# First pass over the weights of k and q: four token tiles of values taken along, weights loaded in pieces, zeros multiplied at the start, first sums copied before the values

## Chip, core and metric

The kernel runs on one core of a Trainium2 chip. A core has five engines that run side by side and wait for each other through semaphores: TensorE (PE, matrix products into PSUM), VectorE (DVE), ScalarE (ACT), GpSimd (POOL) and SyncE (SP, which here only issues transfers). Each engine works through its own queue strictly in order. The metric is the device time of one execution in microseconds (us), lower is better; the figure used is the median of several runs.

## What is computed

One transformer block on 1024 tokens of width 1024, in float32. Only its beginning matters here: a norm, a wide projection, and what the projection's columns are for.

```python
h = rmsnorm(x, g_mix_pre[l])
proj = h @ w_in[l]
qa, ka, va, gate_a, beta_a, alpha_a, qb, kb, vb = jnp.split(proj, split_at, axis=-1)
out_a = gated_deltanet(qa, ka, va, gate_a, beta_a, alpha_a, ...)
out_b = dilated_attention(qb, kb, vb, rel_bias)
mix = jnp.concatenate([out_a, out_b], axis=-1) @ w_out[l]
x = x + rmsnorm(mix, g_mix_post[l])
```

After it comes a gated feed-forward part, which isn't touched.

## The kernel before

**How a product is made.** TensorE gets float32 accuracy from rounded operands: each operand is split into a high part and a low part, and `mm3` adds three products, high by high, high by low and low by high. So each block of weights and of activations is first cast (ACT, the high part) and then subtracted (DVE, the low part). In the names of the profile `wr` is a raw weight block, `w` its parts, `xT` a raw block of the transposed input, `hTh` and `hTl` its parts after multiplication with the norm's gain `gT`. The factor of each token's norm, `rtok`, is put on after the product.

**The first stage.** The depth of 1024 has eight blocks (`KT` = 8, index k). The tokens have two halves of 512 (`hf`), or eight tiles of 128 (t). `proj_first(hf)` runs over k and multiplies block k of the tokens of one half with two chunks of weights, those of head 0 of k and of q (`order[0]` and `order[1]`); their sums stand in the two banks of the pool `pj`. `proj_v(0, tiles)` then makes the values (`bv0`, 256 columns plus 8 columns `wba` for beta and alpha) of four token tiles, each summed over all k in a bank of the pool `pt`, which has four banks and is called `tp` in the profile. The order on TensorE is: half 0 of k and q, value tiles 0 to 3, half 1 of k and q, value tiles 4 to 7, and after that the other chunks.

**What leaves the banks.** `raw_sink(raw, True)` copies a sum of k or q from `pj` to `raw` on ACT, gives the bank back, and later multiplies with `rb` (the norm's factors as a row). A value tile's sink multiplies with `rtok` on ACT (`vs`, `bp`), gives the bank back and stores. `norm_in(t)` makes `rtok`: it squares a tile of x (`xn`, three buffers) on ACT with the sum as a by-product, takes the power on POOL, and after four tiles transposes the four columns on TensorE into a bank of `pt`.

**Loads.** `load_w` is one strand, and all of its transfers are issued by SP in the order in which it yields them: the weights of k and q and the eight `xT` of half 0, `wba`, four blocks of weights for the values, `ident`, four `xn`, the eight `xT` of half 1, and the rest. Raw weights stand in four buffers (`rawS`), `xT` in six. A transfer that needs a buffer waits on SP until that buffer has been used up, and all later transfers wait behind it.

**What sets the order.** A planner (`Weaver`) takes all open strands and always issues the instruction that can start first by its own table of costs; ties go to the strand's priority. `After` holds back a strand until the planner expects its data. `Either` lets the planner choose between two engines. A strand's `slack` tells how long before TensorE would run dry an instruction must be ready by the planner's reckoning to be put into TensorE's queue ahead of others. So the order in each queue is fixed when the kernel is built, and a change at one place can move instructions elsewhere.

Of the kernel before, what the change touches and what calls it, by code (L numbers as in the profile page):

```python
# [48 lines left out]
LATE = 2000.0  # L49
PB = 2  # L50
SW = 832

FAR = {2: 256, 3: 576, 4: 448, 5: 416, 6: 256, 7: 576}
PWO = (2, 3, 2)
# [158 lines left out]
class After:  # L213


    def __init__(self, *aps, late=0.0):
        self.aps, self.late = aps, late


class Strand:  # L220
# [16 lines left out]
class Weaver:  # L237
# [125 lines left out]
    def run(self, *until):  # L363
        while not all(e.set for e in until):
# [15 lines left out]
            for s in live:  # L380
                if s.alts is not None:
                    s.req = s.alts[0]
                    if s.ver >= 0:
                        s.req = min(s.alts, key=lambda r: self.finish(s, r, live))
                names = [x.tensor.name for x in s.req.aps] if isinstance(s.req, After) else \
                    [x[0] for op in s.req for x in op.ins + op.outs]
                v = sum(self.ver.get(n, 0) for n in names)
                if v != s.ver:
                    s.ver = v
                    if isinstance(s.req, After):  # L390
                        s.data = max([t for x in s.req.aps for t, _ in self.wr.get(x.tensor.name, {}).values()] + [0.0])
                    else:
                        s.data = max(self.when(op) for op in s.req)
                if isinstance(s.req, After):
                    s.start, s.safe = s.data + s.req.late, True
                else:
                    free = self.clock[s.req[0].eng]
                    s.start = max(free, s.data, self.port if s.req[0].port else 0.0)
                    if s.req[0].eng == "PE":
                        s.start = max(s.start, self.rest.get(s.gen.__name__, 0.0) if s.pace else 0.0)  # L400
                    if s.req[0].table not in (None, self.table) and not s.eager:
                        s.start += TABLE
                    s.safe = s.req[0].eng != "PE" or s.data + s.slack <= free
                first = min(first, s.start)
# [137 lines left out]
def block_kernel(ctx: ExitStack, tc: tile.TileContext, a, out):  # L542
# [107 lines left out]

    def load_w():

        first = chunks(order[0]) + chunks(order[1])
        got = {c: [] for c in first}
        evs = {c: [Event() for _ in range(2)] for c in first}
        for i in range(2):
            for n, c in enumerate(first):
                wr = yield rawS.get([P, 4, P], F32, name="wr")
                yield SY.dma_start(wr[:], a["w_in"][c][:, 4 * i:4 * i + 4, :])
                got[c].append(wr)  # L660
                evs[c][i].fire()
                if not i:
                    w.spawn(prep_w(c, got[c], evs[c]), 1)
                yield from load_xt(4 * i + n, 0)
                if not i and not n:
                    yield SY.dma_start(gT[:], a["g_mix_pre_t"])
            for k in (2, 3):
                yield from load_xt(4 * i + k, 0)
        yield SY.dma_start(wba[:], a["w_ba"])
        yield from load_item(order[2])  # L670
        yield SY.dma_start(ident[:], a["c_ident"])
        for t in range(4):
            yield from load_x(t)
        for k in range(KT):
            yield from load_xt(k, 1)
        for t in range(4, NT):
            yield from load_x(t)
        ev_x.fire()
        for item in order[3:]:
            yield from load_item(item)  # L680

    def load_item(item):
        for c in chunks(item):
            z, evs = [], [Event() for _ in range(2)]
            for i in range(2):
                wr = yield rawS.get([P, 4, P], F32, name="wr")
                yield SY.dma_start(wr[:], a["w_in"][c][:, 4 * i:4 * i + 4, :])
                z.append(wr)
                evs[i].fire()
            w.spawn(prep_w(c, z, evs), 1)  # L690

    ev_x = Event()
    ev_wh = {(c, i): Event() for c in loaded for i in range(2)}

    def prep_w(c, raw, got):
        hi, lo = [], []
        for i in range(4):
            if c in (24, 25):
                z = yield wS.get([P, 2, WB], F32R, name="w")
            else:  # L700
                z = yield wS.get([P, 4, P], F32R, name="w")
            (lo if i % 2 else hi).append(z)
        wts[c] = hi, lo
        for i, (wh, wl) in enumerate(zip(hi, lo)):
            yield got[i]
            wr = raw[i]
            if c in (24, 25):

                k = 4 * (c - 24) + 2 * i
                yield After(wba[:])  # L710
                yield from split_sb(wh[:, :, 256:], wl[:, :, 256:], wba[:, k:k + 2, :])
                wh, wl, wx = wh[:, :, 0:256], wl[:, :, 0:256], wr[:].rearrange("p (k x) c -> p k (x c)", x=2)
            else:
                wh, wl, wx = wh[:], wl[:], wr[:]
            yield After(wr[:])
            yield from split_sb(wh, wl, wx)
            rawS.put(wr)
            ev_wh[c, i].fire()
        loaded[c].fire()

    def proj_first(hf, sinks):
# [3 lines left out]
        for _ in cs:  # L725
            z = yield pj.get([P, 512], F32, name="pj")
            ps.append(z)
        for k in range(KT):
            for c, z in zip(cs, ps):
                yield ev_wh[c, k // 4]  # L730
                yield ev_xt[k, hf]
                wh, wl = wts[c]
                yield mm3(z[:], wh[k // 4][:, k % 4, :], wl[k // 4][:, k % 4, :], *h_of(k, hf * 512, 512),
                          k == 0, k == KT - 1)
        if hf:
            wS.slots = wS.slots[:8]
            for c in cs:
                wS.put(*wts[c][0], *wts[c][1])
        return [w.spawn(sink(hf, z), 1) for sink, z in zip(sinks, ps)]

    def proj_half(c, hf, sink):
        yield loaded[c]
# [9 lines left out]
    def proj_qk(c0, m, ev):  # L752
# [12 lines left out]
        for hf in range(2):  # L765
            yield from proj_half(c0 + m, hf, sink)

    def proj_v(m, tiles=range(NT)):
        c0 = 24 + 2 * m
        yield loaded[c0]  # L770
        yield loaded[c0 + 1]
        wc = [wts[c0], wts[c0 + 1]]
        n = 256 if m else WB

        def sink(t, ps, bank):
            vs = yield outS.get([P, 4, 64], F32, name="vs")
            yield ev_r[t]
            r = rtok[:, t:t + 1]
            yield A.activation(vs[:], ps[:, 0:256].rearrange("p (h d) -> p h d", h=4), AF.Copy, scale=r)
            if not m:  # L780
                yield A.activation(bp[:, :, t], ps[:, 256:WB], AF.Copy, scale=r)
            (pj if m else pt).put(bank)
            yield SY.dma_start(d_v[t, :, 4 * m:4 * m + 4, :], vs[:])
            outS.put(vs)
            ev_v[m][t].fire()
        for t in tiles:
            if m:
                bank = ps = yield pj.get([P, n], F32, name="pj")
            else:
                bank = yield pt.get([P, 4, P], F32, name="tp")  # L790
                ps = bank[:].rearrange("p k j -> p (k j)")[:, 0:n]
            for k0 in range(0, KT, 2):
                ops = []
                wh, wl = (z[k0 % 4 // 2] for z in wc[k0 // 4])
                for k in (k0, k0 + 1):
                    h, l = (z[:, k % 2, :] if not m else z[:].rearrange("p (k x) c -> p k (x c)", x=2)[:, k % 2, :]
                            for z in (wh, wl))
                    ops += mm3(ps[:], *h_of(k, t * P, P), h, l, k == 0, k == KT - 1)
                yield ops
                if t == NT - 1:  # L800
                    wS.put(wh, wl)
            w.spawn(sink(t, ps, bank), 1)
        if not m and tiles[-1] == NT - 1:
            w.spawn(beta_alpha(ev_v[0]), 2)

# [415 lines left out]
    def raw_sink(raw, early=False):  # L1221
        def sink(hf, ps):
            z, f = raw[0][:, 3 + hf * 512:3 + hf * 512 + 512], rb[:, hf * 512:hf * 512 + 512]
            if early:
                yield A.copy(z, ps[:])
                pj.put(ps)
                yield ev_rb[hf]
                yield Either(*[e.tensor_tensor(z, z, f, ALU.mult) for e in (V, G)])
# [21 lines left out]
    def main():  # L1250
# [5 lines left out]
        for hf in range(2):  # L1256
            evs = yield from proj_first(hf, [raw_sink(raw, True) for raw, _ in pair])
            for (_, ev), e in zip(pair, evs):
                ev.append(e)
            yield from proj_v(0, range(4 * hf, 4 * hf + 4))  # L1260
        ev_v0.fire()
        for n, (kind, i) in enumerate(order):
            if kind in ("k", "q", "v"):
# [30 lines left out]
    with ExitStack() as s0:  # L1294
# [10 lines left out]
        def prep_xt(k, hf, x):  # L1305
# [5 lines left out]
            px.put(x)  # L1311
            ev_xt[k, hf].fire()

        def load_x(t):
            x = yield px.get([P, D], F32, name="xn", bufs=3)
            yield SY.dma_start(x[:], a["x"][t * P:(t + 1) * P, :])
            done_in.append(w.spawn(norm_in(t, x), 1))

        def norm_in(t, x):
            ss = px.tile([P, 1], F32, name="ss%d" % t)  # L1320
# [16 lines left out]
        w.spawn(issue(V.memset(mhalf[:], -0.5)), 0)  # L1337
        wS.more(px, "pw", 8)
        w.spawn(load_w(), 2)
        w.spawn(load_consts(), 3)  # L1340
        ev_main = w.spawn(main(), 9)
        w.run(ev_x)
# [1090 lines left out]
```

## Time and profile before

| what | value |
|---|---|
| median of 3 runs | 1210.13 us (1209.64 to 1210.61) |
| time of the profiled execution | 1212.98 us |
| its span, first to last instruction | 1211.2 us, 19599 instructions |
| TensorE busy | 1194.7 us, 99% of the span |
| VectorE busy | 901.5 us, 74% |
| ScalarE busy | 545.9 us, 45% |
| GpSimd busy | 161.2 us, 13% |
| TensorE's share of the chain that ended last | 85% |

The chain that ended last is found by going back from the last instruction, each time to what released it. TensorE carries most of it. The instructions of a group that sit on it back to back are merged to one row with a count.

### The profile page before, as it was taken

How to read it: one execution, taken by the hardware profiler on the slowest of the kernel's cores; microseconds unless marked ns; L12 is line 12 of the kernel's file. 1: busy time of each engine (PE TensorE's matmuls, PEld its weight loads, DVE VectorE, ACT ScalarE, POOL GpSimd, SP SyncE). 2: the span in 40 equal slices, each digit the busy share in tenths (PEclk: the TensorE clock that was granted, in tenths of full speed). 3: DMA queues.
4: the chain of work that ended last, by engine and by line, in shares of the span. 5: the costliest groups of instructions: out<-in, count | busy, mean ns of one | idle time of the engine just before them, and what ended most of it. 6: DMA issues, size and time to landing. Idle time of an engine off the chain costs nothing.

```text
span 1211.2 us, 19599 instructions
## 1 busy us (share of the span) xinstructions
PE 1194.7 (99%) x7101; PEld 992.5 (82%) x7101; DVE 901.5 (74%) x1729; ACT 545.9 (45%) x1065; POOL 161.2 (13%) x140
## 2 busy tenths in 40 slices
PE   7999999999999999999999999999999999999997
PEld 6978898888888878888788888888888888888886
DVE  4689969636786866676998786787667867876886
ACT  6654531235775764454643333333333344544541
POOL 0143410001111200010101110011100100001111
PEclk9999999999999999999999999999999999999999
DMA  7645363667455344784444433332233239644335
GB/s 257 220 138 181 105 166 109 137 212 272 145 202 187 121 157 161 251 263 164 137 151 139 131 122 122 131 109 69 93 122 122 79 120 338 212 146 140 101 118 208
DMA packets 152216, 192.51 MB, mean 159 GB/s; under 512 B 29960, under 2 KB 77832, under 8 KB 152120
## 3 DMA queue, kind: packets, MB, share of 16 engines
q1 hardware_dynamic: 147896, 189.17, 48.5%
q10 hardware_dynamic: 4224, 2.10, 0.6%
q8 instruction: 56, 0.92, 0.3%
q14 instruction: 40, 0.33, 0.1%
HBM read 135.36 MB, written 59.66 MB: 161 GB/s over the span
## 4 chain that ended last, share of the span: by engine, by line
PE 85%; DVE 7%; DMA 4%; issue 2%; ACT 1%; POOL 1%; SPq 0%; DVEq 0%; POOLq 0%; ACTq 0%
PE bank L286 48%; PE pj L286 21%; PE tp L286 4%; PE p L286 3%; PE pw L286 3%; PE pm L286 2%; PE pS L286 2%; PE pV L286 2%; DVE yc L286 1%; DVE x L286 1%; DMA d_x<-x 1%; DVE wbl L286 1%; DMA ks<-d_k 0%; DMA mx<-d_mix 0%; DMA wraw<-in_w_up 0%
## 5 line engine op out<-in xcount | busy, mean ns | idle before, releaser
L286 PE MATMUL pj<-hTh,w 128*128 128x512 f32 x768 | 263.4, 404 | 6.3 <-ACT hTh L286 6.3
L286 PEld LDWEIGHTS pj<-hTh,w 128*128 128x128 f32 x768 | 145.7, 190 | 40.6 <-ACT hTh L286 6.3
L286 ACT CAST wbh<-wraw 128x512 fp32r<-128x512 f32 x129 | 79.7, 621 | 197.2 <-PE bank L286 116.0
L286 PE MATMUL pj<-hTl,w 128*128 128x512 f32 x384 | 151.5, 395 | 0.0
L286 DVE TENSOR_TENSOR wbl<-wraw,wbh 128x512 fp32r<-128x512 f32 x131 | 92.5, 709 | 29.3 <-ACT wbh L286 29.3
L286 PE MATMUL bank<-views 128*128 128x512 f32 (+1 forms) x307 | 84.8, 384 | 0.0
L286 PEld LDWEIGHTS pj<-hTl,w 128*128 128x128 f32 x384 | 73.1, 190 | 12.7 <-DVE hTl L286 0.5
L286 PE MATMUL bank<-views,dah 128*128 128x512 f32 (+1 forms) x214 | 73.5, 379 | 0.0
L286 PE MATMUL bank<-dbh,views 128*128 128x512 f32 (+1 forms) x201 | 70.3, 380 | 0.0
L286 PEld LDWEIGHTS bank<-views 128*128 128x128 f32 x307 | 57.5, 188 | 11.5
L286 POOL TENSOR_TENSOR m<-m,m 128x512 f32<-128x512 f32 x18 | 28.3, 1572 | 256.3 <-DVE r L286 152.4
L286 ACT CAST w<-wr 128x512 fp32r<-128x512 f32 x55 | 33.8, 620 | 47.8 <-PE pj L286 38.8
L286 PE MATMUL bank<-dbh,dah 128*128 128x512 f32 (+1 forms) x129 | 49.1, 381 | 0.0
L286 DVE SCALAR_TENSOR_TENSOR yc<-raw,convw,yc 128x1024 f32<-128x1024 f32 x36 | 46.5, 1292 | 0.5
L286 PEld LDWEIGHTS bank<-views,dah 128*128 128x128 f32 x214 | 40.0, 188 | 7.7
L286 DVE TENSOR_TENSOR w<-wr,w 128x512 fp32r<-128x512 f32 x42 | 29.1, 700 | 21.9 <-ACT w L286 20.7
L286 PE MATMUL pw<-woh,mh 128*128 128x512 f32 x112 | 44.9, 401 | 0.0
L286 PE MATMUL pw<-woh,ml 128*128 128x512 f32 x112 | 43.8, 391 | 0.0
L286 PE MATMUL pw<-wol,mh 128*128 128x512 f32 x112 | 43.7, 390 | 0.0
L286 PEld LDWEIGHTS bank<-dbh,views 128*128 128x128 f32 x201 | 37.7, 188 | 7.1
L286 DVE TENSOR_TENSOR m<-bank,m 128x512 f32<-128x512 f32 x44 | 30.1, 685 | 17.8 <-PE bank L286 17.6
L286 ACT ACTIVATE Sr<-Sr,mx 128x384 f32<-128x384 f32 (+3 forms) x64 | 38.1, 597 | 9.1 <-DVE mx L286 8.7
(379 smaller groups left out, 3085.6 us busy)
## 6 DMA issues: line engine op xcount, KB each, us to landing
wr<-in_w_in SPq DMA_DIRECT2D x56, 256.0 KB
wraw<-in_w_gate SPq DMA_DIRECT2D x52, 256.0 KB
wraw<-in_w_up SPq DMA_DIRECT2D x52, 256.0 KB
views<-d_hid SPq DMA_DIRECT2D x47, 256.0 KB
db<-in_w_down SPq DMA_DIRECT2D x40, 256.0 KB
da<-d_hid SPq DMA_DIRECT2D x30, 256.0 KB
d_hid<-x SPq DMA_DIRECT2D x22, 256.0 KB
d_hid<-r SPq DMA_DIRECT2D x22, 256.0 KB
```

The costliest lines, as they stand in the source:

```text
L286: op.fn(*op.args, **op.kw)
```

## The change

It has four parts, all in the first 60 us of the program.

1. `proj_first(0)` takes four banks of `pt` at its beginning, and after every second k it also adds that pair's products for value tiles 0 to 3. The value tiles are so summed along with k and q, and the four banks are held all the while. Value tiles 4 to 7 follow after `proj_first(1)`. The strand of the value sinks becomes a function of its own (`v_sink`), spawned after the sinks of k and q.
2. `load_w` loads the weights of k and q in pieces of two k (128x256 instead of 128x512, each with its own event, cast and subtraction), in the order in which the pass needs them, with a block of the values' weights after every second k, and `gT` and `wba` early. `After(..., part=True)` lets a strand wait for one piece of a buffer only.
3. `warm` writes zeros into part of `junk` and multiplies them ten times, 512 columns each, into a bank of `pt` that it takes and gives back.
4. The first sums may be copied by DVE as well as by ACT (`Either`). The strands of `norm_in` get a slack of 5000, which keeps their transposes back on TensorE until they are surely ready.

```diff
+SPREAD = 5000.0
...
-    def __init__(self, *aps, late=0.0):
+    def __init__(self, *aps, late=0.0, part=False):
...
+        yield SY.dma_start(gT[:], a["g_mix_pre_t"])
         first = chunks(order[0]) + chunks(order[1])
...
+        for k in range(0, KT, 2):
+            i, j = k // 4, k % 4
             for n, c in enumerate(first):
+                if not j:
+                    wr = yield rawS.get([P, 4, P], F32, name="wr")
+                    got[c].append(wr)
+                yield SY.dma_start(got[c][i][:, j:j + 2, :], a["w_in"][c][:, k:k + 2, :])
+                evs[c][i][j // 2].fire()
...
+                yield from load_xt(k + n, 0)
+            if not k:
+                yield SY.dma_start(wba[:], a["w_ba"])
+            c = vs[i]
+            wr = yield rawS.get([P, 4, P], F32, name="wr")
+            got[c].append(wr)
+            yield SY.dma_start(wr[:], a["w_in"][c][:, 2 * j:2 * j + 4, :])
...
     def proj_first(hf, sinks):
...
+        vs = []
+        if not hf:
+            for t in range(4):
+                z = yield pt.get([P, 4, P], F32, name="tp")
+                vs.append(z)
         for k in range(KT):
             for c, z in zip(cs, ps):
-                yield ev_wh[c, k // 4]
+                yield ev_wh[c, k // 2]
...
+            if vs and k % 2:
+                yield ev_wh[24 + k // 4, k % 4 - 1]
+                for t, z in enumerate(vs):
+                    yield v_ops(0, t, v_rows(0, z), k - 1)
...
-        return [w.spawn(sink(hf, z), 1) for sink, z in zip(sinks, ps)]
+        evs = [w.spawn(sink(hf, z), 1) for sink, z in zip(sinks, ps)]
+        for t, z in enumerate(vs):
+            w.spawn(v_sink(0, t, v_rows(0, z), z), 1)
+        return evs
...
-                yield A.copy(z, ps[:])
+                yield Either(A.copy(z, ps[:]), V.tensor_copy(z, ps[:]))
                 pj.put(ps)
...
-            yield from proj_v(0, range(4 * hf, 4 * hf + 4))
+        yield from proj_v(0, range(4, NT))
...
+        def warm():
+            tp = yield pt.get([P, 4, P], F32, name="tp")
+            yield V.memset(junk[:, 0:512], 0.0)
+            yield [mm(tp[:].rearrange("p k j -> p (k j)"), junk[:, 0:P], junk[:, 0:512]) for _ in range(10)]
+            pt.put(tp)
...
-            done_in.append(w.spawn(norm_in(t, x), 1))
+            done_in.append(w.spawn(norm_in(t, x), 1, SPREAD))
...
+        w.spawn(warm(), 0)
```

From about the end of value tile 7 on, the five engines' queues hold the same instructions in the same order in both kernels. What moves stands ahead of that.

The first place is ACT's queue where the pass over half 0 ends. Before, the copies of the first sums (`raw<-pj`) stand ahead of the first squares of x (`junk<-xn`) and of all products `hTh` of half 1:

```order
L286 CAST w<-wba 128x2x8
L286 COPY raw<-pj 128x512
L286 CAST w<-wr 128x2x256
L286 COPY raw<-pj 128x512
L286 ACTIVATE junk,ss_267<-xn 128x1024
L286 ACTIVATE junk,ss_273<-xn 128x1024
L286 ACTIVATE vs<-tp,rtok 128x256
```

In the changed kernel the one copy that is left on ACT stands behind four squares and behind all eight `hTh` of half 1:

```order
L287 CAST w<-wr 128x2x256
L287 ACTIVATE junk,ss_300<-xn 128x1024
L287 ACTIVATE junk,ss_311<-xn 128x1024
L287 ACTIVATE junk,ss_319<-xn 128x1024
L287 ACTIVATE junk,ss_365<-xn 128x1024
L287 ACTIVATE hTh<-xT,gT 128x512 x8
L287 COPY raw<-pj 128x512
L287 ACTIVATE vs<-tp,rtok 128x256
L287 ACTIVATE bp<-tp,rtok 128x8
```

The copy moved behind the loads of half 1, and the squares moved ahead of the copy. The other copy stands on DVE behind its eight `hTl`.

The second place is SP's queue between the first weights and the second half. In the changed kernel, at the fourth pair of k (`wr` here is in turn a piece for k, a piece for q and a block for the values):

```order
L287 DMA wr<-in_w_in 128x512
L287 DMA wr<-in_w_in 128x256
L287 DMA xT<-in_x_t 128x512
L287 DMA wr<-in_w_in 128x256
L287 DMA xT<-in_x_t 128x512
L287 DMA wr<-in_w_in 128x512
L287 DMA ident<-in_c_ident 128x128
L287 DMA xn<-in_x 128x1024 x4
L287 DMA xT<-in_x_t 128x512 x8
L287 DMA xn<-in_x 128x1024 x3
```

Before, the values' four blocks stood together behind all `xT` of half 0, and stores of values stood between the `xT` of half 1:

```order
L286 DMA xT<-in_x_t 128x512 x3
L286 DMA wba<-in_w_ba 128x64
L286 DMA wr<-in_w_in 128x512 x4
L286 DMA ident<-in_c_ident 128x128
L286 DMA xn<-in_x 128x1024 x4
L286 DMA xT<-in_x_t 128x512 x2
L286 DMA d_v<-vs 128x256
L286 DMA xT<-in_x_t 128x512 x4
```

The stores left the gaps between the `xT` of half 1, and the weights of the values moved ahead, between those of k and q; four transfers more are issued in all, the eight pieces that stand for four blocks.

The third place is TensorE's queue where half 1 begins, in the changed kernel (the last products of value tile 3, then the first three of k, the transposes of the norms' factors, then q):

```order
L287 MATMUL tp<-w,hTl 128x264
L287 MATMUL pj<-hTh,w 128x512
L287 MATMUL pj<-hTl,w 128x512
L287 MATMUL pj<-hTh,w 128x512
L287 MATMUL tp<-ident,rtok 128x128 x4
L287 MATMUL pj<-hTh,w 128x512
L287 MATMUL pj<-hTl,w 128x512
```

Before, the transposes stood among the products of value tile 3, and the whole of four value tiles stood between the two passes over k and q; now the second pass follows the first with only the last pair's value products between them.

More of the change, by code (lines that the diff above doesn't have):

```diff
@@ L213 @@
 class After:
-    def __init__(self, *aps, late=0.0):
-        self.aps, self.late = aps, late
+    def __init__(self, *aps, late=0.0, part=False):
+        self.aps, self.late, self.part = aps, late, part
 class Strand:
@@ L390, in run @@
                     if isinstance(s.req, After):
-                        s.data = max([t for x in s.req.aps for t, _ in self.wr.get(x.tensor.name, {}).values()] + [0.0])
+                        own = [self.region(x) if s.req.part else (x.tensor.name, -1, -1) for x in s.req.aps]
+                        s.data = max([t for n, q, f in own for (p, g), (t, _) in self.wr.get(n, {}).items() if p & q and f & g] + [0.0])
                     else:
@@ L651, in load_w @@
     def load_w():
+        yield SY.dma_start(gT[:], a["g_mix_pre_t"])
         first = chunks(order[0]) + chunks(order[1])
-        got = {c: [] for c in first}
-        evs = {c: [Event() for _ in range(2)] for c in first}
-        for i in range(2):
-            for n, c in enumerate(first):
[L658 to L662, printed above, removed]
-                    w.spawn(prep_w(c, got[c], evs[c]), 1)
[L664 to L670, printed above, removed]
+        vs = chunks(order[2])
+        got = {c: [] for c in first + vs}
+        evs = {c: [[Event() for _ in range(2)] for _ in range(2)] for c in first}
+        for c in vs:
+            evs[c] = [[Event()] for _ in range(2)]
+        for k in range(0, KT, 2):
+            i, j = k // 4, k % 4
+            for n, c in enumerate(first):
+                if not j:
[4 more added lines that the diff above has]
+                if not k:
+                    w.spawn(prep_w(c, got[c], evs[c]), 1)
+                yield from load_xt(k + n, 0)
+            if not k:
+                yield SY.dma_start(wba[:], a["w_ba"])
[3 more added lines that the diff above has]
+            yield SY.dma_start(wr[:], a["w_in"][c][:, 2 * j:2 * j + 4, :])
+            evs[c][j // 2][0].fire()
+            if not j:
+                w.spawn(prep_w(c, got[c], evs[c]), 1)
         yield SY.dma_start(ident[:], a["c_ident"])
@@ L683, in load_item @@
         for c in chunks(item):
-            z, evs = [], [Event() for _ in range(2)]
+            z, evs = [], [[Event()] for _ in range(2)]
             for i in range(2):
@@ L688, in load_item @@
                 z.append(wr)
-                evs[i].fire()
+                evs[i][0].fire()
             w.spawn(prep_w(c, z, evs), 1)
     ev_x = Event()
-    ev_wh = {(c, i): Event() for c in loaded for i in range(2)}
+    ev_wh = {(c, i): Event() for c in loaded for i in range(4)}
     def prep_w(c, raw, got):
@@ L704, in prep_w @@
         for i, (wh, wl) in enumerate(zip(hi, lo)):
-            yield got[i]
+            yield got[i][0]
             wr = raw[i]
@@ L714, in prep_w @@
                 wh, wl, wx = wh[:], wl[:], wr[:]
-            yield After(wr[:])
-            yield from split_sb(wh, wl, wx)
+            for j, ev in enumerate(got[i]):
+                yield ev
+                x = (slice(None), slice(2 * j, 2 * j + 2) if len(got[i]) > 1 else slice(None))
+                yield After(wx[x], part=len(got[i]) > 1)
+                yield from split_sb(wh[x], wl[x], wx[x])
+                ev_wh[c, 2 * i + j].fire()
             rawS.put(wr)
-            ev_wh[c, i].fire()
         loaded[c].fire()
@@ L766, in proj_qk, with v_rows, v_ops, v_sink @@
             yield from proj_half(c0 + m, hf, sink)
+    def v_rows(m, bank):
+        return bank if m else bank[:].rearrange("p k j -> p (k j)")[:, 0:WB]
+    def v_ops(m, t, ps, k0):
+        c0 = 24 + 2 * m
+        ops = []
+        wh, wl = (z[k0 % 4 // 2] for z in wts[c0 + k0 // 4])
+        for k in (k0, k0 + 1):
+            h, l = (z[:, k % 2, :] if not m else z[:].rearrange("p (k x) c -> p k (x c)", x=2)[:, k % 2, :]
+                    for z in (wh, wl))
+            ops += mm3(ps[:], *h_of(k, t * P, P), h, l, k == 0, k == KT - 1)
+        return ops
+    def v_sink(m, t, ps, bank):
+        vs = yield outS.get([P, 4, 64], F32, name="vs")
+        yield ev_r[t]
+        r = rtok[:, t:t + 1]
+        yield A.activation(vs[:], ps[:, 0:256].rearrange("p (h d) -> p h d", h=4), AF.Copy, scale=r)
+        if not m:
+            yield A.activation(bp[:, :, t], ps[:, 256:WB], AF.Copy, scale=r)
+        (pj if m else pt).put(bank)
+        yield SY.dma_start(d_v[t, :, 4 * m:4 * m + 4, :], vs[:])
+        outS.put(vs)
+        ev_v[m][t].fire()
     def proj_v(m, tiles=range(NT)):
@@ L771, in proj_v @@
         yield loaded[c0 + 1]
[L772 to L785, printed above, removed]
         for t in tiles:
             if m:
-                bank = ps = yield pj.get([P, n], F32, name="pj")
+                bank = yield pj.get([P, 256], F32, name="pj")
             else:
                 bank = yield pt.get([P, 4, P], F32, name="tp")
-                ps = bank[:].rearrange("p k j -> p (k j)")[:, 0:n]
+            ps = v_rows(m, bank)
             for k0 in range(0, KT, 2):
[L793 to L799, printed above, removed]
+                yield v_ops(m, t, ps, k0)
                 if t == NT - 1:
-                    wS.put(wh, wl)
-            w.spawn(sink(t, ps, bank), 1)
+                    wS.put(*(z[k0 % 4 // 2] for z in wts[c0 + k0 // 4]))
+            w.spawn(v_sink(m, t, ps, bank), 1)
         if not m and tiles[-1] == NT - 1:
```

## Prediction

> **What bounds the kernel now.** I read the page first, then the chain that ended last, cut to its first 60 us, then the time lines of TensorE and ACT there, and the table by windows.
>
> ```profile
> span 1211.2 us, 19599 instructions
> PE 1194.7 (99%) x7101; PEld 992.5 (82%) x7101; DVE 901.5 (74%) x1729; ACT 545.9 (45%) x1065; POOL 161.2 (13%) x140
> ...
> 1.64 3.84 DMA gT<-in_g_mix_pre_t
> ...
> 5.57 0.73 ACT hTh L286
> 6.30 0.04 issue
> 6.34 14.44 PE pj L286 x48
> 20.78 12.09 PE tp L286 x100
> 32.87 10.89 PE pj L286 x48
> 43.76 12.08 PE tp L286 x100
> 55.84 5.45 PE pj L286 x24
> ```
>
> TensorE is busy for 99% of the span, so an edit pays only by starting TensorE earlier, by making it faster, or by not stopping it. The chain shows where it loses at the head: nothing runs before 6.34, because the transfer of `gT`, issued third, lands at 5.48 and the first `hTh` follows. From 6.34 on TensorE never stops: 48 products of half 0, four value tiles, 48 of half 1, four value tiles, and at 55.84 the next chunk. But 48 equal products take 14.44 the first time and 10.89 the second. The time line of TensorE shows why (start, duration, instruction):
>
> ```profile
> 7.72 1.05 PE L286 MATMUL pj<-hTh,w 128*128 128x512 f32 x2
> ...
> 9.00 1.05 PE L286 MATMUL pj<-hTh,w 128*128 128x512 f32 x2
> ...
> 12.84 0.66 PE L286 MATMUL pj<-hTh,w 128*128 128x512 f32 x2
> ...
> 19.03 0.61 PE L286 MATMUL pj<-hTh,w 128*128 128x512 f32 x2
> 19.48 0.39 PE L286 MATMUL pj<-hTl,w 128*128 128x512 f32 x1
> 19.71 0.61 PE L286 MATMUL pj<-hTh,w 128*128 128x512 f32 x2
> ```
>
> Three products take 1.28 us (7.72 to 9.00) until 12.84, and 0.68 (19.03 to 19.71) after it. So TensorE ran at about half rate for its first 6.5 us, some 15 products at 0.43 instead of 0.23, which cost 3.1 us. The granted clock of the page shows full speed there; the durations tell it.
>
> **The change, part by part.** The products stay the same; only their order and their start differ. So I ask when half 1 of k and q may begin: that is 32.87 before, and everything behind it follows back to back. Before, the four transposes of the norms' factors stood ahead of that point; now they stand behind the first three products of half 1:
>
> ```profile
> 30.08 0.60 PE L286 MATMUL tp<-ident,rtok 128*128 128x128 f32 x4
> 30.44 0.49 PE L286 MATMUL tp<-w,hTh 128*128 128x264 f32 x2
> ```
>
> They take 0.36 (30.08 to 30.44), so the figure to beat is 32.87 - 0.36 = **32.5 us**.
>
> *Earlier start and zeros.* `gT` goes to the front, and half a block of weights comes with it. Memsets and the first issues stand at 0.7 to 0.9 us, so the zeros can begin at about 1.4; ten of them at the 0.43 of the slow rows take 4.3 us, until 5.7. The first data should be ready near that: `gT` issued first is bounded by the first block's 3.33 below (issue 0.73, 2.6 us for 64 times the bytes) and, above, by its own 5.48 now. I take 5.7 for the first real product, at the price of nothing if the data comes later than that, and of up to 1 us if it is ready at 4.7.
>
> *The pass itself.* At full rate it needs 48 x 0.227 = 10.9 us, and the four value tiles 12.09 - 0.36 = 11.7 (their row of the chain has the transposes in it): 22.6 in all, so 28.3 if nothing waits. I add 0.5 for the first pair of k, where the values' first block must be landed, cast and subtracted behind those of k and q: **28.8 us**. Should the slow rate last as long as before (6.5 us from 1.4, so until 7.9), half of 7.9 - 5.7 is lost, 1.1 us: 29.9.
>
> [...]
>
> *The new wait.* The two banks of `pj` hold the sums of half 0, and half 1 writes the same banks. Before, four value tiles (12 us) lay between, and the copies, the first at 20.14, were hidden under them. Now only the last pair's values lie between, a quarter of 11.7, 2.9 us. And the copies no longer come at once: ACT's stands in its queue behind four squares and all eight `hTh` of half 1, DVE's behind the eight `hTl`. So half 1 can't start before **the last `xT` of half 1 has landed and been worked on**. What that means in time, from ACT, DVE and SP:
>
> ```profile
> 3.33 0.62 ACT L286 CAST w<-wr 128x512 fp32r<-128x512 f32 x1 [1.32 <-DMA wr<-in_w_in]
> ...
> 20.14 0.59 ACT L286 COPY raw<-pj 128x512 f32<-128x512 f32 x1 [3.48 <-PE pj L286]
> ...
> 21.62 1.07 ACT L286 ACTIVATE junk<-xn 128x1024 bf16<-128x1024 f32 x1
> ...
> 34.42 1.34 ACT L286 ACTIVATE hTh<-xT,gT 128x512 fp32r<-128x512 f32 x2
> ```
> ```profile
> 34.38 2.73 DVE L286 SCALAR_TENSOR_TENSOR hTl<-xT,gT,hTh 128x512 fp32r<-128x512 f32 x4
> ...
> 61.57 0.63 DVE L286 TENSOR_TENSOR raw<-pj,rb 128x512 f32<-128x512 f32 x1
> ```
> ```profile
> 13.78 9.36 SPq L286 DMA_DIRECT2D xn<-in_x  x4
> 23.18 0.92 SPq L286 DMA_DIRECT2D xT<-in_x_t  x2
> ```
> ```profile
> 1.00:9.00 8.00, 2.66 (x5) 1.78 (x6) 2.80 (x4) 3.76 (x6) 0.00 (x0) 1.00 0.80 236
> 9.00:14.00 5.00, 5.00 (x15) 3.96 (x14) 4.43 (x7) 4.90 (x8) 0.00 (x0) 1.00 1.04 395
> 14.00:20.00 6.00, 6.00 (x28) 4.94 (x27) 3.17 (x9) 2.22 (x8) 0.00 (x0) 1.00 0.94 325
> 20.00:24.50 4.50, 4.50 (x36) 4.38 (x35) 1.00 (x3) 4.33 (x10) 0.83 (x2) 1.00 0.23 44
> 24.50:33.00 8.50, 8.50 (x72) 8.46 (x71) 3.19 (x7) 6.65 (x13) 1.68 (x4) 1.00 0.93 308
> ```
>
> (The windows' last column is GB/s, the one before it the share of the DMA engines.) There are two ways to work it out.
>
> By bytes: until the last `xT` of half 1 the queue moves 16 blocks of 256 KB, four `xn` of 512 KB, eight `xT` and 0.1 MB of small things, 8.5 MB. At the measured rates 1.9 MB are in by 9 us, 3.9 by 14, and the other 4.6 MB take 14.2 us at 325 GB/s or 14.9 at 308: 28.2 to 28.9. Behind it come one `hTh` (0.73) and one copy (0.59): 29.5 to 30.2, if SP never stops.
>
> By shifting the trace: the last `hTh` of half 1 ends at 35.76 now. In its way was a hole: ACT waited 3.48 us for TensorE with the copy at its head, so the squares began at 21.62 and the fourth `xn`, which needs the first one's buffer, and all `xT` behind it were issued late (SP's row of 9.36 us). From 20 to 24.5 only 44 GB/s moved; at 308 that stretch is worth 3.9 us. In the changed kernel the squares stand ahead of the copy, so this hole closes: 35.76 - 3.9 = 31.9, and with the copy 32.5.
>
> SP adds stops of its own, which the first way leaves out: raw weights have four buffers, now filled in turn for k, q and the values, and from the thirteenth transfer on four of them wait for a subtraction on DVE, with every `xT` behind them on the one queue. One such wait costs at least nothing (others are still in flight) and at most a whole trip, 2.6 us from issue (0.73) to use (3.33). I add 1 us for all four, nearer to nothing, because the transfers issued before a stop go on moving through it. That is 30.5 to 31.2 by bytes and 32.5 by shifting; I take **31.3 us** for the first product of half 1. DVE's copy (nearest row 0.63) comes later than ACT's by one subtraction, 2.73 / 4 = 0.7 us; the three products of k and the transposes ahead of q (0.68 + 0.36) cover that.
>
> So the gain is 32.5 - 31.3 = **1.2 us**, where the earlier start alone would give 3.7.
>
> *The rest.* Smaller pieces cost ACT and DVE four more casts and subtractions each, between 0.3 and 0.7 us apiece; the 3.48 us in which ACT waited hide them, and without that cover they stand in the wait above. Value tiles 4 to 7 need banks that are free long before. Behind 55.84 the queues are the same, TensorE waits next to nothing:
>
> ```profile
> PE pm L286 <- DVE rhd L286: 1.0, 1, 1.0
> PE tp L286 <- ACT ys L286: 0.2, 1, 0.2
> ```
>
> These are all its waits from 56 to 300 us. DVE, which is late there, starts its convolutions no later than TensorE's shift, so I carry the gain through unchanged.
>
> **The rivals.** *No new wait (TensorE's work decides).* If the transfers ran at the 395 GB/s of 9 to 14 us to the end, the other 4.6 MB would take 11.6 us, and the copies would be done at 27; then 28.8 or 29.9 holds, a gain of 3.7 to 2.6 us, 1206.4 to 1207.5. Against it: the trace shows that rate only for 5 us.
>
> *Slower.* SP's stops at the four weight buffers decide. Half 1 starts later than before if the last `xT` lands after 31.2 (32.5 less 0.73 and 0.59), so two full trips of 2.6 on the 28.2 to 28.9 are enough: copies done at 34.7 to 35.4, 2.2 to 2.9 us later than now, about 1212.7. For it: each wait is on an engine that itself waits for a transfer. Against it: transfers in flight cover much of a trip.
>
> *The zeros don't do it.* If zeros do not count as work, or TensorE's waits in the first pair keep its clock down, the slow stretch runs on for 6.5 us from 5.7 and costs 3.1 again: 28.8 + 3.1 = 31.9, a gain of 0.6, 1209.5. It shows little, since the copies come at the same time.
>
> **How the numbers follow.** The profiled execution took 1212.98 us around its span of 1211.2, 2.85 more than the median of 1210.13; the gain of 1.2 goes on either: 1211.8 of a profiled execution, **1208.9** as the median. Chances: the new wait with part of the gain 0.62, no new wait 0.24, slower 0.10, zeros without effect 0.04. 0.2% are 2.4 us, about what a measurement of this kernel can tell from no change; the forecast and the last rival lie within it, the second beyond it, the third about at its other side. So faster 0.24, same 0.66, slower 0.10. The range runs from 1206.6 (the second rival almost whole) to 1211.6 (the stops on SP at half their price).
>
> **What would show it.** The first row of TensorE at about 1.4 us on `junk`, the first real product near 5.7, and durations falling to 0.23 apart by 8. The last `hTh` of half 1 should end near 30.6, right ahead of the copy of `raw`, and TensorE should show one wait on that copy of 1.5 to 2.5 us between its value products and half 1. SP's rows should show stops before the third pair's weights. It is wrong if TensorE has no wait there, or if the next chunk starts elsewhere than at about 54.6 (55.84 less 1.2), or if later waits of TensorE grow.

## The result, and the profile after

| | median us | range, runs | ratio to before (95% interval) |
|---|---|---|---|
| before | 1211.01 | 1209.64 to 1212.38, 6 | |
| changed | **1217.12** | 1216.33 to 1218.67, 6 | 1.0043 (1.0033 to 1.0053) |

The changed kernel is slower by 6.1 us, outside the range and on the other side. The profiled execution took 1217.34 us with a span of 1215.6, against 1212.98 and 1211.2 before. Those two lie only 4.4 us apart, because the profiled execution of before was slower than all six in the table; the 6.1 us are those of the medians.

The loss stands at the head, as the chain that ended last shows for the changed kernel (start, duration, what):

```profile
15.25 5.99 DMA xn<-in_x
...
23.36 5.50 DMA xT<-in_x_t
...
30.42 3.88 DMA xT<-in_x_t
...
34.95 0.57 ACT raw L287
...
35.57 1.65 PE pj L287 x3
37.22 0.85 PE tp L287 x4
38.07 11.18 PE pj L287 x45
49.25 12.08 PE tp L287 x100
61.33 2.73 PE pj L287 x12
```

Before, this chain was TensorE alone from 6.34 on. Now it runs through loads, conversions and the copy `raw` until 35.57, where half 1 of k and q begins. The next chunk starts at 61.33, 5.5 us later than before (55.84), and this offset stays between 4.4 and 6.0 us to the end. The time lines of TensorE and of ACT at the seam:

```profile
29.32 0.28 PE L287 MATMUL tp<-w,hTl 128*128 128x264 f32 x1
35.57 0.80 PE L287 MATMUL pj<-hTh,w 128*128 128x512 f32 x1 [5.96 <-ACT raw L287]
```
```profile
34.32 0.72 ACT L287 ACTIVATE hTh<-xT,gT 128x512 fp32r<-128x512 f32 x1 [1.46 <-DMA xT<-in_x_t]
34.95 0.56 ACT L287 COPY raw<-pj 128x512 f32<-128x512 f32 x1
```

The first pass ends at 29.5, three us sooner than half 1 could start before. Then TensorE stands for 6.0 us, because ACT's copy, which could have been made long before, is queued behind a conversion whose `xT` has not landed. The second loss stands in the table by windows, cut at the steps of the granted clock:

```profile
29.76:33.17 3.41, 0.00 (x0) 0.00 (x0) 3.41 (x6) 3.10 (x5) 0.00 (x0) 1.00 0.75 225
33.17:36.58 3.41, 1.01 (x2) 0.83 (x3) 1.89 (x3) 2.25 (x5) 0.00 (x0) 0.50 0.93 356
36.58:40.00 3.42, 3.42 (x11) 2.73 (x10) 1.43 (x4) 2.88 (x8) 0.55 (x1) 0.50 0.69 232
40.00:43.41 3.41, 3.41 (x16) 2.82 (x15) 0.24 (x3) 3.05 (x9) 1.10 (x2) 1.00 0.98 323
```

(After the length: busy time of PE, PEld, DVE, ACT and POOL with their instructions, then PEclk, DMA share and GB/s.) The stretch from 29.76 holds no product, and from its end at 33.17 the clock is granted at 0.50, until 40.00. Half 1 with the four transposes takes 49.25 - 35.57 = 13.68 us, where 10.91 (run 1 below) and 0.36 would do: 2.4 us. The loss adds up: half 1 starts 35.57 - 32.51 = 3.1 us later, and loses 2.4 more: 5.5.

### The profile page after: what moved, and what is told of

Read it like the earlier page. It is cut to its first block, busy times and chain, and to the rows that moved or that the text cites. A ratio compares the mean times of both kernels' runs of the same rounds, so it can differ in the third digit from the quotient of the medians.

```text
span 1215.6 us, 19641 instructions
## 1 busy us (share of the span) xinstructions
PE 1198.9 (99%) x7111; PEld 993.6 (82%) x7111; DVE 903.8 (74%) x1737; ACT 545.0 (45%) x1066; POOL 161.1 (13%) x140
## 4 chain that ended last, share of the span: by engine, by line
PE 88%; DVE 5%; DMA 3%; issue 1%; ACT 1%; POOL 1%; SPq 0%; DVEq 0%; POOLq 0%; ACTq 0%
PE bank L287 50%; PE pj L287 20%; PE pw L287 6%; PE tp L287 4%; PE p L287 3%; PE pm L287 2%; PE pS L287 2%; PE pV L287 2%; DMA xT<-in_x_t 2%; DVE yc L287 1%; DMA ks<-d_k 1%; DMA xn<-in_x 0%; DVE Sr L287 0%; DVE x L287 0%; SPq L287 0%
## 5 line engine op out<-in xcount | busy, mean ns | idle before, releaser
L287 ACT CAST w<-wr 128x512 fp32r<-128x512 f32 (+1 forms) x58 | 33.9, 590 | 52.6 <-PE pj L287 46.6
L287 DVE TENSOR_TENSOR w<-wr,w 128x512 fp32r<-128x512 f32 (+1 forms) x46 | 29.5, 652 | 16.8 <-ACT w L287 16.0
```

The costliest lines, as they stand in the source:

```text
L287: op.fn(*op.args, **op.kw)
```

## The experiments

Theory A: the order of the queues makes the loss; the copies of the first sums stand behind the conversions of half 1 on ACT and DVE, so half 1 waits for its own loads. Theory B: the loads themselves are late (SP's stops at buffers, the bytes), and half 1 would stand for want of its operands wherever the copies are. Beside them: what the stop costs through the clock, and what each part of the change is worth. The median of before in each set of runs lay between 1211.75 and 1211.87, and was 1211.01 in the set of the result, so times of different sets compare only to about 0.8 us. Every trace is of one execution; those of runs 6 and 7 are the longest of their sets.

**1. Copies first.** The conversions of half 1 are held until both copies have been put into the queues.

```diff
+    ev_copied, copied = Event(), []
...
                 pj.put(ps)
+                copied.append(hf)
+                if len(copied) == 2:
+                    ev_copied.fire()
...
         def prep_xt(k, hf, x):
+            if hf:
+                yield ev_copied
```

> The changed kernel, but the conversions of the half-1 xT are held until both copies of the first sums have been issued, so the copies stand ahead of them on ACT. Theory A (queue order: the copies wait behind eight hTh and hTl, and that alone stops TensorE from 29.5 to 35.6): the stop goes, half 1 starts near 29.7, TensorE stays at full rate, 6.0 + 2.4 us less than the changed kernel, about 1208.7. Rival B (the loads of half 1 are late and TensorE would wait for them in any order): TensorE now stops inside half 1, waiting for hTh or hTl, and less than 3 us come back, about 1214 or more.

Measured: 1209.55 us (1208.31 to 1213.85, 10 runs), ratio to before 0.9984 (0.9973 to 0.9994), 7.6 us less than the change. ACT's time line and the chain:

```profile
26.18 1.24 ACT L287 COPY raw<-pj 128x512 f32<-128x512 f32 x2
27.32 3.80 ACT L287 ACTIVATE hTh<-xT,gT 128x512 fp32r<-128x512 f32 x6
```
```profile
29.71 10.91 PE pj L287 x48
40.62 12.54 PE tp L287 x104
53.16 5.46 PE pj L287 x24
```

The planner now puts both copies on ACT, and the transposes of the norms' factors behind half 1. They are done 2 us before the last pair's values end, and half 1 runs from 29.71 without a stop, though six of its eight conversions come only from 27.32 on and the last two at 33.04. Half 1 uses one block of `xT` every 1.4 us (10.91 us for eight), so it never needed the last one at its start. A holds; B falls as the cause of the stop. The loads of half 1 are hardly earlier here (SP issues its `xT` from 21.80 on, 22.88 in the change); how long the stop of the change lasts does depend on them, as runs 3, 6 and 9 show.

**2. Clock kept up.** In the changed kernel, 24 products of operands that are already there fill a spare bank between the last values and half 1; their sums are not used.

```diff
+        if hf:
+            zb = yield pm.get([P, 512], F32, name="pm")
+            yield [mm(zb[:], hT[0, 0][0][:, 0, 0:P], hT[0, 0][0][:, 0, :]) for _ in range(24)]
+            pm.put(zb)
```

> The changed kernel with 24 products of data that is there (5.4 us, their sum is not used) put on TensorE between the last value products and half 1. Theory A (the stop itself costs 3.1 us against 32.5, and 2.4 us more are lost because TensorE runs half 1's first products at half rate after it): half 1 still starts near 35.6, all its products take 0.23 apart, about 1214.7. Rival C (the rate after a stop isn't set by the idle time): the slow rows stay and the time stays at 1217; if the added products last past the copies, it is longer.

Measured: 1216.54 us (1215.09 to 1217.32, 6 runs), ratio 1.0035 (1.0023 to 1.0047). The chain:

```profile
29.15 5.47 PE pm L287 x24
34.62 6.88 PE pj L287 x30
...
58.15 3.87 PE pj L287 x17
```

The granted clock does not fall, and from the start of half 1 to the next chunk it is 23.5 us and not 25.8, so the fall costs 2.2; with a start 1.0 earlier the next chunk comes 3.2 sooner. The earlier start isn't the edit's doing: no load was touched, but in this execution ACT's copy ends at 34.12 and not at 35.51. So single traces scatter by over a microsecond here. The times show 0.6 us of it (1.0 by the ratios), with intervals that overlap. The trace keeps the 3.1 us until 588 us and then gives them back by 623, two thirds of them at two rows that the change's trace has without a wait:

```profile
621.70 0.50 PE L287 MATMUL bank<-T2h,wbh 128*128 128x512 f32 x1 [1.08 <-ACT wbh L287]
622.92 0.50 PE L287 MATMUL bank<-T2h,wbl 128*128 128x512 f32 x1 [0.49 <-DVE wbl L287]
```

A weight transfer of the feed-forward part (7.22 us) lands late there, ahead of ACT's and DVE's work on it. Why it is late in this run wasn't followed up. So the clock's part is shown in the trace of the head, not in the time.

**3. Eight buffers for `xT`** in the changed kernel, two of them taken from another pool, the queues' order kept.

```diff
-            x = yield px.get([P, 512], F32, name="xT", bufs=6)
+            x = yield xtS.get([P, 512], F32, name="xT")
...
+        xtS = Slots(px, "xs", 6)
+        xtS.slots += outS.slots[:2]
```

> The changed kernel with eight buffers for xT instead of six (two are borrowed from the stores' buffers, which are idle then); the order of all queues is the same. Theory A1 (the last two xT of half 1 are late because SP waits for a buffer until the first hTl of half 1 is done, issues at 28.8 and 30.4): they are issued by 26.5, the last lands 1 to 2 us before 34.3, and half 1 starts that much earlier, about 1215.5. Rival D (the transfers fill the DMA queues anyway): the last one lands at 34.3 as before, 1217.

Measured: 1215.92 us (1214.7 to 1216.55, 8 runs), ratio 1.003 (1.002 to 1.0041). The chain:

```profile
28.46 3.93 ACT hTh L287 x6
32.39 0.48 ACT raw L287
...
32.92 1.65 PE pj L287 x3
...
58.13 3.87 PE pj L287 x17
```

The stop shrinks from 6.0 to 3.2 us, and the clock is at half for one stretch of 3.4 us instead of two. SP's rows, first of the changed kernel, then of this run:

```profile
22.88 7.87 SPq L287 DMA_DIRECT2D xT<-in_x_t  x8
```
```profile
22.25 4.07 SPq L287 DMA_DIRECT2D xT<-in_x_t  x8
```

So the last two `xT`, which in the change were issued only when a conversion had given back a buffer, account for some 2.65 us of the late start (32.92 against 35.57, one trace each).

**4. Zeros alone**, on the kernel before.

```diff
+        def warm():
+            tp = yield pt.get([P, 4, P], F32, name="tp")
+            yield V.memset(junk[:, 0:512], 0.0)
+            yield [mm(tp[:].rearrange("p k j -> p (k j)"), junk[:, 0:P], junk[:, 0:512]) for _ in range(10)]
+            pt.put(tp)
...
+        w.spawn(warm(), 0)
```

> The kernel before with the ten zero products alone, nothing else of the change. Theory A (the zeros are worth the 15 slow products, 3.1 us, and nothing of the loss comes from them): about 3 us less than before, 1208; products 0.23 apart from the first on except where hTh is late. Rival E (zeros don't raise the rate, or they hold up the first products): no change, 1211, or slower.

Measured: 1216.44 us (1213.74 to 1220.66, 10 runs), ratio 1.0038 (1.0024 to 1.0051): the expectation missed. The time line of TensorE:

```profile
23.97 0.32 PE L286 MATMUL tp<-ident,rtok 128*128 128x128 f32 x1 [0.28 <-POOL rtok L286]
26.03 0.32 PE L286 MATMUL tp<-ident,rtok 128*128 128x128 f32 x1 [1.74 <-POOL rtok L286]
...
27.90 0.64 PE L286 MATMUL tp<-w,hTh 128*128 128x264 f32 x2
```

The planner, whose reckoning the zeros shift too, put the transposes of `rtok` ahead of norms that are not there yet. TensorE waits 2.0 us, and from 27.33 the clock is at half for 3.41 us, another 1.7. That puts the next chunk at 57.45, 1.6 us later than before. The median lies 4.6 above; the profiled execution (1214.54) was one of the quicker, and what the other runs lost is open.

**5. Copies first, without the zeros.** One line less than in 1 (`w.spawn(warm(), 0)`), and the same order around the seam.

> The version with the copies ahead of half 1's conversions, and without the ten zero products; the order on every engine stays as in that version. Theory (the zeros buy clock): the clock is granted only some 6.5 us after the first real product, as in before (6.34 to 12.91), so about half of 6.5 us of products is lost, 3 us: half 1 starts near 32.7 and not 29.7, the next chunk near 56 and not 53.2, the time near 1212.5. Rival (the first pass waits for its loads, so the zeros are without effect): within 1 us of the version with the zeros, 1209.5 to 1210.5, with PE waits of 2 to 3 us in the first pass of the version with zeros, which its trace does not show.

Measured: 1210.34 us (1209.09 to 1211.63, 11 runs), ratio 0.9986 (0.9978 to 0.9995). The chain:

```profile
5.14 5.53 PE pj L287 x12
...
30.56 10.91 PE pj L287 x48
```

The time falls in the rival's range, the trace between both: the zeros are worth 0.85 us at the start of half 1 (30.56 against 29.71), not 3 and not nothing. The first real product comes at the same time (5.14 here, 5.17 with zeros), and the clock is full at 10.17 instead of 5.82. The first twelve products take 5.4 us here (to 10.51) and 3.8 with the zeros (to 9.01), where 2.7 would do at full rate; with the zeros one of them waits for `hTl`, and the first value products for their weights until 9.60. So most of what the clock gives is not used. The times (0.8 apart) don't separate the two.

**6. Six raw weight buffers** in the changed kernel's first pass.

```diff
+        rawS.slots += outS.slots[2:]
...
         ev_x.fire()
+        rawS.slots = rawS.slots[:4]
```

> The change with six raw weight buffers in the first pass in place of four, so that SyncE does not stop at the third pair's weights; the order of ScalarE, VectorE and SyncE stays the change's. If SyncE's stops at the weight buffers set the end of the loads (the prediction's rival with two trips), the last transposed tile of half 1 lands some 2.6 us earlier or more, half 1 starts near 31 to 33 and the time is 1212 to 1214. If they do not, because the last tiles wait for their six buffers and the bytes ahead of them are the same, half 1 starts within 1 us of 35.6 and the time is 1216 to 1217.5.

Measured: 1215.43 us (1214.82 to 1217.6, 6 runs), ratio 1.0032 (1.0021 to 1.0043). SP's rows, first of the changed kernel, then of this run:

```profile
5.91 3.34 SPq L287 DMA_DIRECT2D wr<-in_w_in  x2
...
15.25 7.59 SPq L287 DMA_DIRECT2D xn<-in_x  x4
```
```profile
5.91 0.91 SPq L287 DMA_DIRECT2D wr<-in_w_in  x2
...
13.05 6.96 SPq L287 DMA_DIRECT2D xn<-in_x  x4
```

Without the stop at the third pair's weights the `xn` go out 2.2 us earlier, and ACT's copy ends at 33.18 instead of 35.51. Half 1 starts at 34.91, between the two expectations, since here the transposes of `rtok` came to stand ahead of it, and waited for a bank:

```profile
33.45 0.27 ACT L287 ACTIVATE bp<-tp,rtok 128x8 f32<-128x8 f32 x1
```
```profile
33.83 1.09 PE L287 MATMUL tp<-ident,rtok 128*128 128x128 f32 x4 [4.07 <-issue]
```

The view names no releaser, but the last reader of a value bank (`bp`) ends at 33.72, 0.1 us before them: most likely again work that gives back a bank, behind the conversions in ACT's queue.

**7. Zeros alone with the slack** of the change for the norms, on the kernel before.

```diff
+SPREAD = 5000.0
...
-            done_in.append(w.spawn(norm_in(t, x), 1))
+            done_in.append(w.spawn(norm_in(t, x), 1, SPREAD))
```

> The kernel before with the ten zero products and with the change's slack of 5000 for the norms: the first transposes of rtok stand 24 rows later in TensorE's order than in the run with the zeros alone. If the early transposes made that run slow, there is no wait for rtok of over 0.3 us, the clock does not fall, the next chunk starts near 53 and the time is 1208 to 1210. If the zeros alone are worth nothing in the order of before, because the loads of the first pass and half 1 come too late for a faster TensorE, the next chunk starts at 55.5 to 57.5 and the time is 1211 to 1214.

Measured: 1213.46 us (1210.62 to 1216.07, 12 runs), ratio 1.0009 (1.0001 to 1.0017). Time and next chunk (57.13) are those of the expectation's second case, but not for its reason: the transposes stand later and no longer wait for `rtok`, but, it seems, for a bank (the view names no releaser; a `bp` ended at 29.69):

```profile
29.78 0.62 PE L287 MATMUL tp<-ident,rtok 128*128 128x128 f32 x4 [1.98 <-issue]
```
```profile
26.93:30.35 3.42, 1.44 (x13) 1.26 (x12) 2.20 (x4) 2.96 (x7) 0.00 (x0) 1.00 0.96 323
30.35:33.76 3.41, 3.41 (x18) 3.41 (x17) 3.19 (x5) 3.41 (x9) 0.00 (x0) 0.50 0.94 283
```

The first value products stand at 18.34 here and at 20.78 before, 2.4 us gained; the stop of 2.0 and half of 3.4 us at half clock take 3.7, and half 1 starts at 34.12. A stop of 2.0 us was enough for the clock to fall, after TensorE had begun to work again. So in the order of before a faster first pass is given back at the transposes, with the slack as without it.

**8. Copies first, values not taken along**, four tiles behind each half as in before.

```diff
-        if not hf:
+        if not hf and 0:
             for t in range(4):
...
+            yield from proj_v(0, range(4 * hf, 4 * hf + 4))
...
-        yield from proj_v(0, range(4, NT))
```

> The version with the copies ahead, in which the value tiles are not taken along in the first pass but follow it, four by four, as in before. If taking them along is what keeps TensorE fed while the loads come, there are waits of 1.5 to 3 us for the loads in the first pass, half 1 starts near 31 to 32.5 and the time is 1210.5 to 1212.5. If not, half 1 starts near 29.7 and the time is 1209 to 1210.

Measured: 1214.09 us (1212.06 to 1215.3, 11 runs), ratio 1.0017 (1.0009 to 1.0026). The time line of TensorE:

```profile
5.46 0.50 PE L287 MATMUL pj<-hTh,w 128*128 128x512 f32 x1
...
16.29 0.51 PE L287 MATMUL pj<-hTh,w 128*128 128x512 f32 x1 [1.09 <-ACT hTh L287]
...
21.41 0.41 PE L287 MATMUL tp<-w,hTh 128*128 128x264 f32 x2
```

The 48 products take 16.0 us (5.46 to 21.41) and not 10.9. The waits that the view names, all for `hTh` or `hTl`, come to 2.5 us of the 5.1; the rest is wider spacing at rows without a named wait. Half 1 starts at 33.66, 4 us later than with the values along and later than expected, and the time is 4.5 above run 1. So with the copies first, this part of the change earns the most: value products fill the time in which the loads come.

**9. Both relaxations of the buffers** (3 and 6 together) in the changed kernel.

> The change with both relaxations, six raw weight buffers and eight buffers for transposed tiles, the order of ScalarE and VectorE as in the change. If the two were separate parts of the late loads, what they gave adds up: ScalarE's copy of the first sums ends near 31 (35.5 in the change, 33.2 and near 33 with one of them), half 1 starts near 32, the clock falls for one stretch of 3.4 us or for none, and the time is 1213 to 1214.5. If one cause stands behind both (the bytes ahead of the last tile), half 1 starts at 32.7 or later, as with the eight buffers alone, and the time is 1214.5 to 1216.

Measured: 1214.79 us (1212.14 to 1216.48, 10 runs), ratio 1.0019 (1.0009 to 1.0029). ACT's time line and the chain:

```profile
30.88 0.57 ACT L287 COPY raw<-pj 128x512 f32<-128x512 f32 x1
```
```profile
30.10 1.99 issue
32.09 0.62 PE tp L287 x4
32.71 12.52 PE pj L287 x48
```

The copy ends at 31.45, 4.1 us earlier than in the change; one relaxation alone gave 2.6 (`xT`) and 2.3 (weights), so the two are separate for the most part. The start of half 1 then hangs on the transposes again, most likely on their bank (a `bp` ends at 31.99), and the clock falls for 3.4 us. The copy is where the first case put it; the start of half 1 (32.71) and the time fall in the second.

**10. Copies first, with both relaxations.**

> The version with the copies ahead and with both relaxations of the buffers. If the loads still cost something once the copies go first, the next chunk starts before 53.2 and the time is under 1209. If TensorE already works without a stop there (no wait over 0.3 us after the first pass in the version without the buffers), nothing is left to gain: the next chunk at 53.0 to 53.6 and the time 1209 to 1210.5.

Measured: 1209.84 us (1209.42 to 1212.02, 11 runs), ratio 0.9984 (0.9975 to 0.9994); half 1 starts at 29.48 and the next chunk at 52.92, against 29.71 and 53.16 in 1. Once the copies go first, earlier loads have nothing left to give.

Versions 1, 5 and 10 beat both kernels, by 1.5 to 2.3 us against before and by some 7 against the change.

## Why the prediction was wrong

- **The figure to beat** (half 1 at 32.5) was right as a measure: the start of half 1 and what follows it make up the whole 5.5 us at the next chunk.
- **Earlier start, zeros, the pass.** The zeros began at 1.28 (about 1.4 foreseen), and the pass ended at 29.5 (28.8). That ten zeros would be enough, 28.8 and not 29.9, no trace had shown; it was right: the clock is full at 5.87, and run 5 puts their worth at 0.85 us. That this is near the 1.1 of the sum is luck, for without them the half rate lasts until 10.17, and most of what it costs there would be spent waiting for loads anyway.
- **The new wait** was seen where it stands and with its reason: run 1 changes nothing but the order of the queues, and the wait is gone. Its size failed. The first product was to come at 31.3 and came at 35.57.
- **The step that failed** is "I add 1 us for all four, nearer to nothing", SP's stops, with its reason that the transfers issued before a stop go on moving through it. Only one of the four cost much, and it alone took 2.4 us (SP's row of 3.34, where run 6 has 0.91). Transfers in flight did not fill it: from 9 to 14 us the changed kernel moved 248 GB/s where the sum by bytes put 395, 0.7 MB less; run 6, without the stop, moved 373. The delay was passed on. `xn` was issued at 15.25 (13.78 before), the squares could begin only when it landed, at 21.34 (21.62 before), the fourth `xn` needed the first one's buffer, and so the `xT` of half 1 were issued from 22.88 on, hardly sooner than before (23.18). So the second way, which let this hole close for 3.9 us, failed as well: from 20 to 24.5 us 181 GB/s moved and not 308, another 0.6 MB. In run 6 the `xn` go out at 13.05, the squares begin at 18.51, and the `xT` go out from 20.11 on.
- **A second stop was left out:** six buffers of `xT` for eight blocks. SP's row for the eight takes 7.87 us, and 4.07 with eight buffers (run 3). The copy of ACT ends at 35.51, 2.3 us earlier without the first stop, 2.6 without the second and 4.1 without both, at 31.45. That this is close to the forecast of 31.3 is in part luck: the hole from 20 to 24.5 stays even then (193 GB/s in run 9), and a faster stretch behind it makes up for it (413 from 29 to 33).

```profile
9.00:14.00 5.00, 5.00 (x34) 4.50 (x33) 4.32 (x9) 3.50 (x9) 0.39 (x1) 1.00 0.82 248
...
20.00:24.50 4.50, 4.50 (x33) 4.22 (x32) 0.36 (x3) 3.01 (x5) 1.11 (x2) 1.00 0.58 181
```
```profile
21.34 1.06 ACT L287 ACTIVATE junk<-xn 128x1024 bf16<-128x1024 f32 x1 [2.18 <-DMA xn<-in_x]
```

- **The rival named "Slower"** had the right kind of mechanism, a stop of SP at the weight buffers, and its place for the copies, 34.7 to 35.4, is near the measured 35.51. The nearness is partly luck: it counted two trips at the weight buffers, where one stop there and one at the buffers of `xT` did it. It got 0.10, and its time of 1212.7 was still too low, because **a term was missing**: the prediction took for granted that half 1 runs at full rate after the wait. The stop of 6.0 us took the clock with it, 2.4 us more (2.2 in run 2, which fills the stop). A slow rate was weighed there for the start only, where the trace of before shows 6.5 us of it behind 6.3 us without a product. Whether a stop at the seam would bring it back was not asked; the windows above show that it did (29.76 to 33.17 without a product, then 0.50).
- **54.6 for the next chunk** was thus 6.7 too early: 4.3 from the size of the wait, 2.4 from the clock.
- **The rest** held: behind the next chunk the offset to before doesn't grow by more than 0.5 us and ends smaller, so no later wait adds to the loss.

## What to carry to other kernels

A copy that frees a bank must not stand in an in-order queue behind work that waits for a load, or TensorE waits for that load too, although it needs it much later (6.0 us in the changed kernel, no wait there in run 1); look for it wherever the distance between two uses of a bank shrinks. When pausing TensorE is part of a forecast, price the pause twice, once for its length and once for the clock after it (here 6.0 us and 2.4). Don't count on transfers in flight to cover a stop of the issuing queue at a full buffer: 2.4 us of it delayed the loads behind by 2.2 here. And count the buffers of everything that queue fills, not only of what the change adds.

## What the runs showed of the hardware

In these traces the granted clock changed at steps that lie whole multiples of 3.41 us apart, on a grid: in the changed kernel it was full from 5.87 to 33.17 (eight times 3.41) and at half until 40.00 (twice, and twice in run 6); in runs 3, 4, 7 and 9 the half rate lasted 3.41 us, once. It fell at the end of a stretch of the grid that was empty (the changed kernel), in which TensorE was busy for 1.44 us of 3.42 (run 7) or for 1.63 of 3.42 (run 4), and it held through one with 2.47 of 3.41 (run 8). First run 4, then run 8:

```profile
23.91:27.33 3.42, 1.63 (x12) 1.44 (x13) 1.57 (x3) 3.32 (x7) 0.55 (x2) 1.00 0.93 322
```
```profile
15.65:19.06 3.41, 2.47 (x8) 1.54 (x9) 2.79 (x7) 3.41 (x8) 0.00 (x0) 1.00 1.00 356
```

So the fall came when TensorE was at work again (run 7: work from 29.78, fall at 30.35), and the stretch ahead of it was not always empty: run 7's was 42% busy, run 4's 48%. Run 8's, with no fall after it, was 72% busy, and in the kernel before the clock held through a stretch with 2.31 of 3.41 (from 582.94, 68%); what happens between 48% and 68% was not measured. Stops of 2.0 us (runs 4, 7 and 9) and of 3.2 (run 3) were followed by 3.41 us at half, those of 4.1 (run 6) and 6.0 (the changed kernel) by 6.83. That the price of a stop depends also on how it lies on the grid is an estimate from these shares: 2.0 us, cut in half by a step, would leave 71% of either stretch busy, near the 72% of run 8.
